# Two heads side by side in the array: neighbourhood units of a pair of heads and two-head score products in a hybrid encoder kernel

## The chip, the cores and the metric

The kernel runs on one core of a Trainium2 chip. The metric is device time in microseconds (us), the median of some runs; beside it there is one execution taken by the hardware profiler. Engines: PE is the tensor engine (its matmuls), DVE the vector engine, ACT the scalar engine, POOL and SP mainly issue transfers here. PSUM is the memory that PE writes; it has eight banks of 512 floats in each of 128 partitions.

## What is computed

Two layers over 512 tokens of width 1024 in float32. Each layer is a half-step SwiGLU feed-forward, a mixer with two kinds of heads, and a second feed-forward; a final norm follows.

```python
def hybrid_layer(x, ...):
    x = x + 0.5 * swiglu(rmsnorm(x, ffn1_norm), ffn1_wg, ffn1_wu, ffn1_wd)
    proj = rmsnorm(x, mix_norm) @ w_in          # all heads' q, k, v, gates
    na_o = rmsnorm(merge_heads(neighbourhood_attention(...)), na_gain)
    o_fwd = gla_chunked(qg, kg, vg, log_gf, True)
    o_bwd = flip(gla_chunked(flip(qg), flip(kg), flip(vg), flip(log_gb), False))
    gla_o = merge_heads(rmsnorm(o_fwd + o_bwd, gla_gain)) * silu(g_r)
    x = x + concatenate([na_o, gla_o]) @ w_out
    return x + 0.5 * swiglu(rmsnorm(x, ffn2_norm), ffn2_wg, ffn2_wu, ffn2_wd)
```

Neighbourhood attention has 8 heads of width 64: a query on the 8 x 64 grid of tokens sees a window of 8 x 16, with a learned bias per head, and a softmax over it. Gated linear attention (GLA) has 4 heads with keys of width 64 and values of width 128; the score of a query and a key is their product, damped by the gates between them, in both directions.

## The kernel before

Every activation lies with its features on the 128 partitions and the 512 tokens along the row. A projection is done as three products of rounded high and low parts (`mm3`, L165), with the weight quarters split by ACT and DVE shortly before (`split`, L144). These products, 0.23 us apart at 512 columns, are the bulk of the work.

The mixer (`mixer`, L530) emits four streams that `interleave` (L502) puts in one order, by what each step says it takes on PE and how long its successor must wait: `gla_all(0)` and `gla_all(1)` for the two pairs of GLA heads, `na_all` for the neighbourhood heads, and `fillers`, the projections of the next heads and then the first part of the output projection. LVL, SCL, NAP are such waiting times, in planned us. A scheduler in the framework then moves instructions of each engine once more within what dependencies allow, so that the order on an engine isn't quite that of the code.

Two heads share a tile of q and k: head 0 of the pair in partitions 0 to 63, head 1 in 64 to 127. A product for one head thus fills 64 of PE's 128 rows.

GLA (`gla_levels`, L596) builds its scores in levels. For the levels up to 64 tokens, `scores` (L625) takes for one head eight products of 64 x 64 (`blocks`, L619, L623), with odd blocks in the lower half of the output's partitions, and merges them into `atc` by a masked copy on DVE (L633), or by ACT for the first and the last level (L630, L688). Between levels four DVE products (L659, L660, L665, L666) scale keys and queries by the gates. The 128 level is four products of 128 columns a head (L697), the 256 level two halves of two products of 256 columns (L711); ACT copies them out (L700, L715).

A neighbourhood unit (`na_unit`, L828) is half of the query columns of one head: two score products of 256 columns (L846), bias and maximum on DVE (L851), exponentials on ACT (L855), the division (L860), four transposes (L864), ACT's copy out (L866), and four products with the values that write 64 partitions of the tile `po` (L874). Its bias comes by two POOL transfers a head (L834, L835). `na_all` (L890) keeps up to three units in flight.

PSUM is divided into pools: four banks "mm" for the projections, two banks "sc" for all scores, one "tp" for transposes and row sums, one "o" for `po`. A score step of one head takes one of the two "sc" banks and gives it back when its scores are read.

Every fp32 product is two records in the trace: a step of eight products shows as x16.

Of the kernel before, what the change touches and what calls it, by code (L numbers as in the profile page):

```python
# [9 lines left out]
F32 = mybir.dt.float32  # L10
# [15 lines left out]
SCL = 1.31  # L26
HEAD = 9
# [5 lines left out]
NAP = 5.46  # L33
# [27 lines left out]
def trunk_kernel(ctx, tc, xin, wgu, wdn, win, wcode, wgate, wout, vec, rpbt,  # L61
# [68 lines left out]
    # the tensor engine's clock comes up while the first data are on their way  # L130
# [106 lines left out]
    def rsqrt_row(ps, n, t, r, a, act=False):  # L237
        # 1/sqrt(mean + eps): exp(-ln/2) as a start, then one Newton step
# [116 lines left out]
    def ffn(l, which):  # L355
# [27 lines left out]
        def direct_pairs(hid):  # L383
            # the first weight tiles, while the row scales are on their way
# [93 lines left out]
    def last_row(pss, hs):  # L478
        # the last two chunks and the row scales of the final norm, for one half of the tokens
# [50 lines left out]
    def mixer(l):  # L530
# [3 lines left out]
        # gate codes: both parts of the weights side by side, summed by the gate product  # L534
# [11 lines left out]
        def codes():  # L546
            # both copies of the codes; then the first as high parts, the second as low parts
# [48 lines left out]
        def gla_levels(pr):  # L596
# [22 lines left out]
            def blocks(ps, op):  # L619
                # the eight blocks of 64 tokens, odd ones in the lower half of the rows  # L620
                for i in range(8):
                    o = (i % 2) * 64
                    PE.matmul(ps[o:o + 64, (i // 2) * 64:(i // 2 + 1) * 64], *op(i), start=True, stop=True)  # L623

            def scores(hh, kk, qf, li):  # L625
                ps = psum("sc")
                blocks(ps, lambda i: (kk[hh * 64:hh * 64 + 64, i * 64:(i + 1) * 64], qf(i)))
                dst = atc[:, hh * H2:(hh + 1) * H2]
                if li is None:
                    S.activation(dst, ps[:, :H2], AF.Copy)  # L630
                else:
                    m = lms[:, li, :].rearrange("p (a t) -> p a t", a=1).broadcast_to([P, 4, 64])
                    V.copy_predicated(dst.rearrange("p (b t) -> p b t", b=4), m,  # L633
                                      ps[:, :H2].rearrange("p (b t) -> p b t", b=4))

            for hh in range(2):
                scores(hh, ka, lambda i: qa[hh * 64:hh * 64 + 64, i * 64:(i + 1) * 64], None)
                yield 0.7, SCL
            for hh in range(2):
                scores(hh, ka, lambda i: qop(hh, i, 1), 0)  # L640
                yield 0.7, SCL
            for li, h in enumerate((1, 2, 4, 8, 16, 32, 64, 128)):
# [25 lines left out]
                if h2 <= 32:  # L668
                    for hh in range(2):
                        scores(hh, kc, lambda i: qop(hh, i, h2), li + 1)  # L670
                        yield 0.7, SCL
                elif h2 == 64:
                    for hh in range(2):
                        b = hh * 64
                        ps = psum("sc")

                        def halves(i):
                            kk, qq = (KF, QF) if i % 2 == 0 else (KB, QB)
                            return (kk[b:b + 64, i * 64:(i + 1) * 64],
                                    qq[b:b + 64, (i ^ 1) * 64:((i ^ 1) + 1) * 64])  # L680

                        blocks(ps, halves)
                        at.append(sl("at", F32, f"g{pr}"))
                        av = at[hh].rearrange("p (b two t) -> p two b t", b=4, two=2)
                        for o in range(2):
                            rows = slice(o * 64, o * 64 + 64)
                            for src, k in ((atc[rows, hh * H2:(hh + 1) * H2], o), (ps[rows, :H2], 1 - o)):
                                S.activation(av[rows, k], src.rearrange("p (b t) -> p b t", b=4), AF.Copy)  # L688
                        yield 0.7, SCL
                elif h2 == 128:  # L690
                    for hh in range(2):
                        b = hh * 64
                        ps = psum("sc")
                        for s in range(4):
                            t = s ^ 1
                            kk, qq = (KF, QF) if s < t else (KB, QB)
                            PE.matmul(ps[:, s * P:(s + 1) * P], kk[b:b + 64, s * P:(s + 1) * P],  # L697
                                      qq[b:b + 64, t * P:(t + 1) * P], start=True, stop=True)
                        g["m", hh] = sl("am", F32, f"g{pr}")
                        S.activation(g["m", hh], ps, AF.Copy)  # L700
                        yield 0.9, SCL
                else:
                    for hh in range(2):
                        b = hh * 64
                        for half in range(2):
                            ps = psum("sc")
                            kk, qq = (KF, QF) if half == 0 else (KB, QB)
                            o = 256 * (1 - half)
                            for j in range(2):
                                s = 2 * half + j  # L710
                                PE.matmul(ps[:, j * 256:(j + 1) * 256],  # L711
                                          kk[b:b + 64, s * P:(s + 1) * P], qq[b:b + 64, o:o + 256],
                                          start=True, stop=True)
                            g["f", hh, half] = sl("af", F32, f"g{pr}")
                            S.activation(g["f", hh, half], ps, AF.Copy)  # L715
                        yield 1.8, 0.5
# [65 lines left out]
        # neighbourhood attention  # L782
        def vmat_steps(pss, src, tags):
            # the values with the tokens as rows: the chunks' token blocks times two weight tiles
# [43 lines left out]
        def na_unit(hp, hh, jp, ctxd):  # L828
            hd = 2 * hp + hh
            b = hh * 64  # L830
            q, k = got["qk", hp]
            if jp == 0:
                nb0, nb1 = sl("nb", F32, "na"), sl("nb", F32, "na")
# [303 lines left out]
```

## Time and profile before

| | |
|---|---|
| median of three runs | 1989.24 us (1986.94 to 1990.84) |
| profiled execution, span | 1989.2 us |
| PE busy | 1969.5 us |
| DVE busy | 1423.7 us |
| ACT busy | 1025.6 us |
| TensorE clock granted, mean | 0.996 of full speed |

The profiled execution's span is that of all its instructions; the runs around it have the same time. A share of busy time is a mean over feed-forward and mixer stages. The mixer of layer 0 lies between some 362 and 658 us, that of layer 1 between 1342 and 1639.

### The profile page before, as it was taken

To read this page: it belongs to the slowest core of one execution; us is meant where nothing else is said; L and a number is where in the kernel's file an instruction comes from. 1 tells how busy PE (TensorE), PEld (TensorE's weight loads), DVE (VectorE), ACT (ScalarE), POOL (GpSimd) and SP (SyncE) were. 2 spreads that over 40 slices of the span, in tenths; PEclk is the share of its full clock that TensorE was granted. 3 is DMA by queue.
4 is the path that set the end of the run, shared out by engine and by line. 5 is a ranking of instruction groups with operands and counts; after the bars stand their busy time and mean duration, and the time that the engine had idled before them with its cause. 6 is when DMAs were issued, how large, how long until landed. Compare 5 with 4: busy or idle time off the path is not lost.

```text
span 1989.2 us, 32211 instructions
## 1 busy us (share of the span) xinstructions
PE 1969.5 (99%) x12490; PEld 1717.5 (86%) x12490; DVE 1423.7 (72%) x2745; ACT 1025.6 (52%) x1959; POOL 17.5 (1%) x36
## 2 busy tenths in 40 slices
PE   8999999999999999999999999999999999999997
PEld 7889999878778898999889898988777888999896
DVE  6958767666549985967787596775664689769585
ACT  5535535455555552644555364554554555536364
POOL 0000000000000000000000000000000000000000
PEclk9999999999999999999999999999999999999999
DMA  4332323222112332232223232223221133323322
GB/s 152 113 109 101 107 98 109 93 72 68 65 38 65 118 109 93 105 107 101 97 100 106 90 105 104 101 93 106 78 70 35 46 101 103 107 100 110 108 78 74
DMA packets 57737, 185.69 MB, mean 93 GB/s; under 512 B 6640, under 2 KB 13296, under 8 KB 45296
## 3 DMA queue, kind: packets, MB, share of 16 engines
q1 hardware_dynamic: 29904, 132.07, 19.4%
q10 hardware_dynamic: 25632, 45.27, 7.0%
q0 software_dynamic: 2048, 6.29, 1.0%
q8 instruction: 98, 1.61, 0.3%
q14 instruction: 55, 0.45, 0.1%
HBM read 181.51 MB, written 2.10 MB: 92 GB/s over the span
## 4 chain that ended last, share of the span: by engine, by line
PE 97%; DVE 1%; DMA 1%; ACT 0%; issue 0%; DVEq 0%; ACTq 0%
PE F_mm L166 14%; PE F_mm L168 14%; PE F_mm L167 14%; PE F_sc L166 9%; PE F_sc L167 9%; PE F_sc L168 9%; PE M_mm L166 6%; PE M_mm L168 6%; PE M_mm L167 6%; PE M_sc L623 2%; PE M_o L874 2%; PE M_sc L846 2%; PE M_tp L864 1%; PE M_sc L711 1%; PE M_mm L768 1%; DMA wraw<-in_wgu 0%
## 5 line engine op out<-in xcount | busy, mean ns | idle before, releaser
L146 ACT ACTIVATE F_wh<-F_wraw 128x512 fp32r<-128x512 f32 (+1 forms) x472 | 290.3, 618 | 453.7 <-PE F_sc L167 242.2
L166 PE MATMUL F_mm<-F_xc,F_wh 128*128 128x256 f32 x1792 | 500.7, 282 | 1.7 <-ACT F_wh L146 1.7
L167 PE MATMUL F_mm<-F_xc,F_wh 128*128 128x256 f32 x1792 | 501.5, 281 | 0.0
L168 PE MATMUL F_mm<-F_xc,F_wl 128*128 128x256 f32 x1792 | 495.0, 282 | 0.0
L147 DVE TENSOR_TENSOR F_wl<-F_wraw,F_wh 128x512 fp32r<-128x512 f32 (+1 forms) x472 | 313.3, 670 | 154.3 <-ACT F_wh L146 149.2
L166 PEld LDWEIGHTS F_mm<-F_xc,F_wh 128*128 128x128 f32 x1792 | 339.3, 190 | 4.3 <-ACT F_wh L146 2.5
L167 PEld LDWEIGHTS F_mm<-F_xc,F_wh 128*128 128x128 f32 x1792 | 340.3, 190 | 1.9
L168 PEld LDWEIGHTS F_mm<-F_xc,F_wl 128*128 128x128 f32 x1792 | 335.6, 190 | 0.0
L166 PE MATMUL F_sc<-F_hid,F_wh 128*128 128x512 f32 (+1 forms) x716 | 275.6, 387 | 1.3 <-DVE xt L452 1.3
L167 PE MATMUL F_sc<-F_hid,F_wh 128*128 128x512 f32 (+1 forms) x716 | 276.6, 386 | 0.0
L168 PE MATMUL F_sc<-F_hid,F_wl 128*128 128x512 f32 (+1 forms) x716 | 276.4, 386 | 0.0
L146 ACT ACTIVATE F_wh<-F_ws 128x512 fp32r<-128x512 f32 x256 | 162.3, 634 | 166.7 <-PE F_mm L167 106.9
L147 DVE TENSOR_TENSOR F_wl<-F_ws,F_wh 128x512 fp32r<-128x512 f32 x256 | 174.9, 688 | 41.8 <-ACT F_wh L146 38.6
L166 PEld LDWEIGHTS F_sc<-F_hid,F_wh 128*128 128x128 f32 x716 | 134.5, 188 | 28.9 <-DVE xt L452 3.0
L168 PEld LDWEIGHTS F_sc<-F_hid,F_wl 128*128 128x128 f32 x716 | 134.5, 188 | 26.5
L167 PEld LDWEIGHTS F_sc<-F_hid,F_wh 128*128 128x128 f32 x716 | 134.6, 188 | 25.7
L452 DVE SCALAR_TENSOR_TENSOR xt<-F_sc,xt 128x512 f32<-128x512 f32 x94 | 65.0, 692 | 97.0 <-PE F_sc L168 96.4
L166 PE MATMUL M_mm<-F_xd,M_wh 128*128 128x512 f32 x304 | 122.2, 403 | 0.0
L167 PE MATMUL M_mm<-F_xd,M_wh 128*128 128x512 f32 x304 | 120.6, 398 | 0.0
L168 PE MATMUL M_mm<-F_xd,M_wl 128*128 128x512 f32 x304 | 120.5, 397 | 0.0
L147 DVE TENSOR_TENSOR M_wl<-M_wraw,M_wh 128x512 fp32r<-128x512 f32 (+1 forms) x112 | 73.4, 668 | 36.3 <-ACT M_wh L146 23.1
L146 ACT ACTIVATE M_wh<-M_wraw 128x512 fp32r<-128x512 f32 (+1 forms) x112 | 67.7, 615 | 55.4 <-PE M_mm L167 37.6
(327 smaller groups left out, 3247.5 us busy)
## 6 DMA issues: line engine op xcount, KB each, us to landing
F_wraw<-in_wgu SPq DMA_DIRECT2D x64, 1024.0 KB, 4.8
F_wraw<-in_wdn SPq DMA_DIRECT2D x32, 1024.0 KB, 4.9
M_wraw<-in_win ACTq DMA_DIRECT2D x88, 256.0 KB, 3.6
F_wraw<-in_wgu ACTq DMA_DIRECT2D x80, 256.0 KB, 3.6
F_wraw<-in_wdn SPq DMA_DIRECT2D x16, 768.0 KB, 4.2
M_nb<-in_rpbt POOLq DMA_DIRECT2D x16, 256.0 KB, 3.0
M_wraw<-in_wout SPq DMA_DIRECT2D x16, 256.0 KB, 2.7
xt<-in_xin SPq DMA_DIRECT2D x8, 256.0 KB, 5.0
```

The lines of the kernel that those rows point to most:

```text
L146: S.activation(h, src, AF.Copy)
L147: V.tensor_tensor(l, src, h.bitcast(F32), op=ALU.subtract)
L166: PE.matmul(ps, wh, rh, start=first, stop=False, skip_group_check=more)
L167: PE.matmul(ps, wh, rl, start=False, stop=False, skip_group_check=more)
L168: PE.matmul(ps, wl, rh, start=False, stop=last, skip_group_check=more)
L452: V.scalar_tensor_tensor(xt[:, c, :], pss[j], 0.5, xt[:, c, :], ALU.mult, ALU.add)
L623: PE.matmul(ps[o:o + 64, (i // 2) * 64:(i // 2 + 1) * 64], *op(i), start=True, stop=True)
L711: PE.matmul(ps[:, j * 256:(j + 1) * 256], kk[b:b + 64, s * P:(s + 1) * P], qq[b:b + 64, o:o + 256], start=True, stop=True)
L768: PE.matmul(dst, vs(2 * half + j), fa[:, o:o + P], start=False, stop=(j == 1))
L846: PE.matmul(pss[:, jj * 256:(jj + 1) * 256], q[b:b + 64, j * P:(j + 1) * P], krhs, start=True, stop=True)
L864: PE.transpose(pt[:, i * P:(i + 1) * P], pp[:, i * P:(i + 1) * P], idn)
L874: PE.matmul(po[b:b + 64, j * P:(j + 1) * P], got["v", hp][VSEL[j][c]][:, hh * 64:(hh + 1) * 64], pT[:, (jj * 2 + c) * P:(jj * 2 + c + 1) * P],
```

## The change

All score steps, and the whole neighbourhood unit, are done for two heads at once. In `blocks` the two heads alternate product by product, each with its own "sc" bank; the masked copies follow for both. The 128 and 256 levels do the same. A neighbourhood unit is now half of the query columns of both heads of a pair (`na_unit(hp, jp, ...)`): four score products that alternate between the heads, then both softmaxes, two groups of transposes, and eight value products that alternate between the upper and the lower half of `po`. There are eight units a layer in place of sixteen. The bias of a unit is loaded one unit ahead by `na_load` into the very tile that DVE then writes the biased scores to; the copy of `po` into `nao` is gone, and the split and the squares read the bank. NAP, now for two heads, is 10.4 in place of 5.46; FAL, NAX and NAT are further planned waits.

```diff
-NAP = 5.46
+NAP = 10.4
+FAL = 1.4
+NAX = 0.0
+NAT = 0.3
...
-            def blocks(ps, op):
+            rows = slice(0, 64), slice(64, P)
+            def blocks(pss, op):
                 for i in range(8):
                     o = (i % 2) * 64
-                    PE.matmul(ps[o:o + 64, (i // 2) * 64:(i // 2 + 1) * 64], *op(i), start=True, stop=True)
-            def scores(hh, kk, qf, li):
-                ps = psum("sc")
...
+                    for hh in range(2):
+                        PE.matmul(pss[hh][o:o + 64, (i // 2) * 64:(i // 2 + 1) * 64], *op(hh, i),
+                                  start=True, stop=True)
+            def scores(kk, qf, li):
+                pss = psum("sc"), psum("sc")
+                blocks(pss, lambda hh, i: (kk[rows[hh], i * 64:(i + 1) * 64], qf(hh, i)))
+                for hh, ps in enumerate(pss):
+                    dst = atc[:, hh * H2:(hh + 1) * H2]
...
                 if h2 <= 32:
-                    for hh in range(2):
-                        scores(hh, kc, lambda i: qop(hh, i, h2), li + 1)
-                        yield 0.7, SCL
+                    scores(kc, lambda hh, i: qop(hh, i, h2), li + 1)
+                    yield 0.8, SCL
...
                 elif h2 == 128:
+                    pss = psum("sc"), psum("sc")
+                    for s in range(4):
+                        t = s ^ 1
+                        kk, qq = (KF, QF) if s < t else (KB, QB)
+                        for hh in range(2):
+                            PE.matmul(pss[hh][:, s * P:(s + 1) * P], kk[rows[hh], s * P:(s + 1) * P],
+                                      qq[rows[hh], t * P:(t + 1) * P], start=True, stop=True)
...
+                    for half in range(2):
+                        pss = psum("sc"), psum("sc")
...
+                            for hh in range(2):
+                                PE.matmul(pss[hh][:, j * 256:(j + 1) * 256],
+                                          kk[rows[hh], s * P:(s + 1) * P], qq[rows[hh], o:o + 256],
                                           start=True, stop=True)
...
+        def na_load(hp, jp):
+            pps = []
+            for hh in range(2):
+                pp = sl("pp", F32, "na")
+                nc.gpsimd.dma_start(pp, rpbt[l, 2 * hp + hh, :, jp * H2:jp * H2 + T])
+                pps.append(pp)
+            return pps
+        def na_unit(hp, jp, pps, ctxd):
             q, k = got["qk", hp]
+            sco = psum("sc"), psum("sc")
...
             for jj in range(2):
                 j = 2 * jp + jj
+                for hh in range(2):
...
+                    PE.matmul(sco[hh][:, jj * 256:(jj + 1) * 256], q[rows[hh], j * P:(j + 1) * P], krhs,
+                              start=True, stop=True)
+            for ps, pp in zip(sco, pps):
+                sm = small(4)
+                for jj, cs in enumerate(halves):
+                    V.tensor_tensor_reduce(pp[:, cs], ps[:, cs], pp[:, cs],
...
+                V.tensor_scalar(sm[:, 0:2], sm[:, 0:2], -1.0, None, ALU.mult)
+                for jj, cs in enumerate(halves):
+                    S.activation(pp[:, cs], pp[:, cs], AF.Exp, bias=sm[:, jj:jj + 1],
...
+            for pp in pps:
+                pt = psum("tp")
+                for i in range(4):
+                    PE.transpose(pt[:, i * P:(i + 1) * P], pp[:, i * P:(i + 1) * P], idn)
+                S.activation(pp, pt, AF.Copy)
+                yield 0.6, NAT
...
+                    v = got["v", hp][VSEL[j][c]]
+                    for hh in range(2):
+                        PE.matmul(po[rows[hh], j * P:(j + 1) * P], v[:, rows[hh]],
+                                  pps[hh][:, (jj * 2 + c) * P:(jj * 2 + c + 1) * P],
+                                  start=(c == 0), stop=(c == 1))
...
-                V.tensor_copy(nao := sl("nao", F32, "na"), po)
-                osplit(nao, hp, lvec(l, hp))
+                osplit(po, hp, lvec(l, hp))
```

What stands in a row on the engines, at the places that the prediction speaks of. A row is line, operation, output tile<-inputs, shape and repetition; tiles carry a running number, and line numbers are each program's own.

PE before, one GLA level of the second pair in layer 0: `M_sc` is a score bank, one for each head, `M_ga` and `M_kt` hold the scaled queries and keys, `M_mm` is a filler's bank.

```order
L864 MATMUL M_tp_4892<-con,M_pp_4781 128x128 x4
L623 MATMUL M_sc_4902<-M_ga_4649,M_kt_4772 64x64 x8
L623 MATMUL M_sc_4936<-M_ga_4649,M_kt_4772 64x64 x8
L167 MATMUL M_mm_4853<-M_wl_4837,F_xd_3611 128x256
L168 MATMUL M_mm_4853<-M_wh_4836,F_xd_3611 128x256
```

The same level after the change, on PE, as far as its fourth piece (the alternation goes on in ones up to eight blocks a head).

```order
L169 MATMUL M_mm_4776<-M_wh_4771,F_xd_3827 128x256
L170 MATMUL M_mm_4776<-M_wl_4772,F_xd_3827 128x256
L630 MATMUL M_sc_4868<-M_ga_4630,M_kt_4744 64x64 x2
L630 MATMUL M_sc_4869<-M_ga_4630,M_kt_4744 64x64 x2
L630 MATMUL M_sc_4868<-M_ga_4630,M_kt_4744 64x64
L630 MATMUL M_sc_4869<-M_ga_4630,M_kt_4744 64x64
```

The sixteen blocks of the two heads were eight and eight; now they alternate.

PE before, the last 64-token level of the second pair, layer 0: `M_tp` is the transpose bank; some 25 more rows of fillers follow before the 128 level (L697).

```order
L168 MATMUL M_mm_5747<-F_xd_3834,M_wl_5764 128x512
L623 MATMUL M_sc_5692<-M_ga_4649 64x64 x8
L728 MATMUL M_tp_5784<-con,M_vt_5725 128x128
L623 MATMUL M_sc_5728<-M_ga_4649 64x64 x8
L728 MATMUL M_tp_5784<-con,M_vt_5725 128x128 x3
L166 MATMUL M_mm_5748<-F_xd_3834,M_wh_5770 128x512
```

The same place after: L701 is the 128 level, L715 the 256 level, L876 transposes and L887 value products of the last neighbourhood unit.

```order
L171 MATMUL M_mm_5801<-F_xd_3834,M_wl_5824 128x512
L630 MATMUL M_sc_5700<-M_ga_4630 64x64 x8
L630 MATMUL M_sc_5701<-M_ga_4630 64x64 x8
L876 MATMUL M_tp_5734<-con,M_pp_5501 128x128 x4
L701 MATMUL M_sc_5865<-M_ga_4630 128x128 x4
L701 MATMUL M_sc_5866<-M_ga_4630 128x128 x4
L876 MATMUL M_tp_5750<-con,M_pp_5503 128x128 x4
L887 MATMUL M_o_5762<-M_pp_5501,M_vm_4993 64x128
L715 MATMUL M_sc_6005<-M_ga_4630 128x256 x2
L715 MATMUL M_sc_6006<-M_ga_4630 128x256 x2
```

The last filler stands ahead of the three levels, which now follow each other with a group of transposes or a single product between them.

ACT at that place after the change: L693 fills the tiles `M_at` from the score banks and from `M_atc`, L705 and L720 copy the 128 and 256 levels out, L877 the transposes.

```order
L693 ACTIVATE M_at_5718<-M_sc_5700 64x4x64 x2
L693 ACTIVATE M_at_5723<-M_atc_4633 64x4x64 x2
L693 ACTIVATE M_at_5723<-M_sc_5701 64x4x64 x2
L877 ACTIVATE M_pp_5501<-M_tp_5734 128x512
L705 ACTIVATE M_am_5875<-M_sc_5865 128x512
L705 ACTIVATE M_am_5877<-M_sc_5866 128x512
L877 ACTIVATE M_pp_5503<-M_tp_5750 128x512
L720 ACTIVATE M_af_6011<-M_sc_6005 128x512
L720 ACTIVATE M_af_6013<-M_sc_6006 128x512
```

The second head's bank is read after six of the copies; before, the copies from `M_atc` stood earlier in ACT's order and only four stood here.

## Rows read from the trace of the kernel before

**Rows 1.** The page: busy time by engine (share, instructions); the chain by engine

```profile
PE 1969.5 (99%) x12490; PEld 1717.5 (86%) x12490; DVE 1423.7 (72%) x2745; ACT 1025.6 (52%) x1959; POOL 17.5 (1%) x36
...
PE 97%; DVE 1%; DMA 1%; ACT 0%; issue 0%; DVEq 0%; ACTq 0%
```

**Rows 2.** Stretches: us; busy of PE, PEld, DVE, ACT, POOL; clock; DMA share; GB/s

```profile
400.00:500.00 100.00, 100.00 (x824) 79.74 (x823) 63.66 (x201) 55.16 (x129) 4.29 (x8) 1.00 0.22 69
500.00:590.00 90.00, 90.00 (x607) 68.14 (x606) 44.40 (x123) 45.20 (x92) 2.15 (x4) 1.00 0.17 57
590.00:658.00 68.00, 67.91 (x339) 56.87 (x338) 56.12 (x93) 37.02 (x65) 0.00 (x0) 1.00 0.24 78
```

**Rows 3.** Chain of work, layer 0: start us, us until the next piece, what

```profile
408.19 0.81 PE M_sc L623 x16
...
415.93 1.06 PE M_sc L846 x4
...
434.51 1.02 PE M_o L874 x8
...
453.92 0.91 PE M_sc L623 x30
...
539.81 1.08 PE M_sc L697 x8
...
565.92 0.61 PE M_sc L623 x16
...
570.67 0.23 PE M_mm L167
...
572.97 1.64 PE M_sc L697 x16
...
581.43 1.92 PE M_sc L711 x8
```

**Rows 4.** Timeline of PE around a score group: start us, us, instruction

```profile
415.53 0.28 PE L167 MATMUL M_mm<-M_wl,F_xd 128*128 128x256 f32 x1
415.65 0.28 PE L168 MATMUL M_mm<-M_wh,F_xd 128*128 128x256 f32 x1
415.86 1.13 PE L846 MATMUL M_sc<-M_k,M_q 64*128 64x256 f32 x4
416.91 0.50 PE L166 MATMUL M_mm<-F_xd,M_wh 128*128 128x512 f32 x1
417.25 0.40 PE L167 MATMUL M_mm<-F_xd,M_wh 128*128 128x512 f32 x1
```

**Rows 5.** Timeline of PE where two heads' score steps meet

```profile
454.30 0.22 PE L623 MATMUL M_sc<-M_ga,M_kt 64*64 64x64 f32 x1
454.31 0.22 PE L623 MATMUL M_sc<-M_gq,M_gk 64*64 64x64 f32 x1
```

**Rows 6.** Timeline of PE where a 128 level meets a neighbourhood group

```profile
534.93 0.82 PE L697 MATMUL M_sc<-M_ga 64*128 64x128 f32 x5
535.49 0.48 PE L846 MATMUL M_sc<-M_k,M_q 64*128 64x256 f32 x1
535.59 0.38 PE L697 MATMUL M_sc<-M_ga 64*128 64x128 f32 x2
```

**Rows 7.** The page's DMA issues: the bias, count, KB each, us to landing

```profile
M_nb<-in_rpbt POOLq DMA_DIRECT2D x16, 256.0 KB, 3.0
```

**Rows 8.** Timeline of DVE: two passes over a head's neighbourhood scores

```profile
469.35 0.42 DVE L851 CUSTOM_DVE_ANT_0 M_pp<-M_sc,M_nb 128x256 f32<-128x256 f32 x1
...
469.70 0.42 DVE L851 CUSTOM_DVE_ANT_0 M_pp<-M_sc,M_nb 128x256 f32<-128x256 f32 x1
```

**Rows 9.** Timeline of DVE: first and last of a level's four products

```profile
566.57 0.43 DVE L659 TENSOR_TENSOR M_ga<-M_ga,M_pk 128x256 f32<-128x256 f32 x1
...
567.58 0.42 DVE L666 TENSOR_TENSOR M_ga<-M_ga,M_pk 128x256 f32<-128x256 f32 x1
```

**Rows 10.** Timeline of ACT: four copies of a 64-token step

```profile
565.71 1.67 ACT L688 ACTIVATE M_at<-M_sc 64x256 f32<-64x256 f32 x4
```

More of the change, by code (lines that the diff above doesn't have):

```diff
@@ L642, in gla_levels @@
+            scores(ka, lambda hh, i: qa[rows[hh], i * 64:(i + 1) * 64], None)
+            yield 0.8, SCL
+            scores(ka, lambda hh, i: qop(hh, i, 1), 0)
+            yield 0.8, SCL
             for li, h in enumerate((1, 2, 4, 8, 16, 32, 64, 128)):
@@ L668, in gla_levels, with halves @@
                 if h2 <= 32:
-                    for hh in range(2):
-                        scores(hh, kc, lambda i: qop(hh, i, h2), li + 1)
-                        yield 0.7, SCL
+                    scores(kc, lambda hh, i: qop(hh, i, h2), li + 1)
+                    yield 0.8, SCL
                 elif h2 == 64:
[L673 to L682, printed above, removed]
+                    pss = psum("sc"), psum("sc")
+                    def halves(hh, i):
+                        kk, qq = (KF, QF) if i % 2 == 0 else (KB, QB)
+                        return (kk[rows[hh], i * 64:(i + 1) * 64],
+                                qq[rows[hh], (i ^ 1) * 64:((i ^ 1) + 1) * 64])
+                    blocks(pss, halves)
+                    for hh, ps in enumerate(pss):
                         at.append(sl("at", F32, f"g{pr}"))
@@ L690, in gla_levels @@
+                    yield 0.8, SCL
                 elif h2 == 128:
-                    for hh in range(2):
[L692 to L698, printed above, removed]
+                    pss = psum("sc"), psum("sc")
@@ L701, in gla_levels @@
-                        yield 0.9, SCL
-                else:
[L703 to L712, printed above, removed]
+                        S.activation(g["m", hh], pss[hh], AF.Copy)
@@ new lines, in gla_levels @@
+                    yield 1.0, SCL
+                else:
+                    for half in range(2):
+                        pss = psum("sc"), psum("sc")
+                        kk, qq = (KF, QF) if half == 0 else (KB, QB)
+                        o = 256 * (1 - half)
+                        for j in range(2):
+                            s = 2 * half + j
+                            for hh in range(2):
+                                PE.matmul(pss[hh][:, j * 256:(j + 1) * 256],
+                                          kk[rows[hh], s * P:(s + 1) * P], qq[rows[hh], o:o + 256],
@@ new lines, in na_unit @@
+            for sm, pp in zip(sms, pps):
+                V.reciprocal(sm[:, 2:4], sm[:, 2:4])
+                for jj, cs in enumerate(halves):
+                    V.tensor_scalar(pp[:, cs], pp[:, cs], sm[:, 2 + jj:3 + jj], None, ALU.mult)
+            yield 1.0, NAX
+            for pp in pps:
[4 more added lines that the diff above has]
+                yield 0.6, NAT
@@ L869, in na_unit @@
+            if jp == 0:
                 ctxd["po"] = psum("o")
@@ L884, in na_unit @@
                 else:
-                    sq = sl("sq", F32, "na")
+                    sq = sl("sq", F32, "ws")
                     S.activation(sq, po, AF.Square)
                     V.tensor_tensor(st["nacc"], st["nacc"], sq, op=ALU.add)
-            yield 0.9, 0.0
+            yield 1.1, 0.0
         def na_all():
             ctxd = {}
-            act = []
-            for u in range(16 + DEEP):
-                if u < 16:
-                    hp = u // 4
-                    yield ("qk", hp)
-                    yield ("v", hp)
-                    act.append(na_unit(hp, (u // 2) % 2, u % 2, ctxd))
-                left = NAP
-                for gq in act[::-1]:
-                    y = next(gq, None)
-                    if y is not None:
-                        left -= sum(y)
-                        yield y
-                act = act[-DEEP:]
+            units = []
+            pps = na_load(0, 0)
+            for u in range(8 + DEEP):
+                if u < 8:
+                    yield ("qk", u // 2)
+                    yield ("v", u // 2)
+                    units.append(na_unit(u // 2, u % 2, pps, ctxd))
+                left = NAP if u < 8 else 3.0
+                for age, n in enumerate((1, 2, 1)):
+                    if 0 <= u - age < 8:
+                        for _ in range(n):
+                            y = next(units[u - age])
+                            left -= sum(y)
+                            yield y
+                if u < 7:
+                    pps = na_load((u + 1) // 2, (u + 1) % 2)
                 yield 0.0, max(left, 0.0)
```

85 lines of the change are left out of this document (23 added, 62 removed).

## The prediction

> **What bounds the kernel now.** I read the page first: TensorE (PE) is busy for 99% of the span and the chain of work that ended last runs on PE for 97% of it [rows 1]. Then the table of stretches, because only the mixer is touched: between 400 and 658 us (layer 0, whose mixer starts at some 362 us; layer 1 is the same 980 us later) PE is busy for all but 0.1 us, while DVE is at 49 to 83% and ACT at 50 to 55% [rows 2]. So in the stage that changes the time is the sum of PE's start-to-start steps, and whatever shortens these shortens the run until another engine comes late. The chain gives that sum directly: a piece of the chain is the time from the first start of a group to the first start of what follows [rows 3].
>
> Two things are to be seen in these pieces. First, a small group pays for changing the shape of the array. In [rows 4] products with 256 columns start every 0.12 us, but 0.21 us pass before the first product of 64 rows; after it the first full one holds PE for 0.34 us, where such products otherwise take 0.23 [rows 3]. That is about 0.09 + 0.11 us on the neighbours of each small group, beside a late first step and a late last step that its own piece contains. Second, products in different parts of the array run together already. A step of one head (16 records of 64x64) takes 0.61 us; two heads that happen to stand back to back take 0.91 and not twice 0.61 [rows 3], and where the first head's last blocks meet the second head's first, records of both start within 0.01 us [rows 5]. The same holds for row halves with 128 columns: a neighbourhood product starts at 535.49 while the level products of the other half go on every 0.11 us, and two heads of L697 take 1.64 instead of twice 1.08 [rows 3, 6]. Two products of the same half don't: L711 x8 takes 1.92 against 1.06 for the four records of the same shape in L846 [rows 3].
>
> **The change, part by part (both layers).** In the reordered program the two heads alternate product by product in nearly all steps, so I take a two-head step at the price of the one-head step.
>
> GLA steps of 64x64. Before: 64 one-head steps, 8 of them with the strided operand of the first level at 0.81, the others 32 alone at 0.61 and 24 in 12 adjacent pairs at 0.91: 6.5 + 19.5 + 10.9 = 36.9 us. After: 32 steps; 26 at 0.62, 4 strided at 0.82, and 2 (the last level of the second pair, where the order has eight blocks of one head and then eight of the other) at 0.91: 16.1 + 3.3 + 1.8 = 21.2. Saved 15.7.
>
> Neighbourhood scores. 32 groups at 1.06 become 16 of the same length: saved 17.0.
>
> Values (L874). 32 groups at 1.02 = 32.6. After, the two heads fill the two column halves, so 16 groups of eight products need 1.02 each where they stand whole; the order cuts ten of them into 1 + 7 and two into 3 + 5, and a cut costs about 0.36: 16 x 1.02 + 12 x 0.36 = 20.6. Saved 12.0. The trace before has no two 128x64 products of different column halves next to each other. The bounds are 0, if they run one after another (then 11 us of the 12 stay), and the full 12; I take the full value, since the blocks of L623 also go to alternating column halves of one bank and start in pairs.
>
> Levels 128 and 256. L697: eight one-head groups, four alone at 1.08 and two adjacent pairs at 1.64, 7.6 us; after, two at 1.64 (four products of one head, then four of the other) and two better mixed at about 1.35: 6.0. L711: 16 half-level groups, 16.5 us with their adjacent ones (eight at 1.06, two runs of 1.92, the rest 4.2); after, the order leaves eight groups of one head alone, with fillers between the heads, at 1.06, and pairs four: 12.7. Saved 1.6 + 3.8.
>
> Neighbours. The number of changes between the full array and a small shape falls from 124 to 86 by the order: 38 x 0.19 = 7 us.
>
> Sum: 15.7 + 17.0 + 12.0 + 1.6 + 3.8 + 7 = 57 us less for PE.
>
> Off PE: the eight copies of the finished head pair out of its bank go (0.69 us of DVE each), and the bias is loaded into the tile that becomes the probabilities. That makes 32 loads of 256 KB in place of 16 of that size and 16 of half; they land in 3.0 us [rows 7] and are issued a unit, some 16 us of PE work, ahead. I cost both at nothing; what hides the loads is that distance, and without it each unit would pay up to 3 us.
>
> **What comes late next.** PE takes its instructions in order, so a product that waits holds all fillers behind it. Every two-head step now needs both score banks, so both heads of the step before must have been read. In the middle of the mixer the order leaves 3.2 to 5 us of PE work between such steps. Reading two neighbourhood heads takes four DVE passes that start 0.34 us apart [rows 8], about 1.9 us with the hand-overs; that fits unless DVE is behind. I put 1 us per layer on it, bounds 0 and 5.
>
> The end of the second pair's levels is different. Before, some six us of fillers lie between the 64-token step and the 128 step (565.92 and 572.97), and between that and the 256 step (581.43) [rows 3]. In the new order the fillers are used up by then, and 0.7 us of PE work separates the first two and 0.7 us the next. But each level first needs four DVE products on the result of the one before, 1.4 us from first start to last end [rows 9], and the 128 step needs both banks, for which ACT has six copies of 0.4 us in its queue [rows 10]: 2.4 us. So PE waits about 2 us at the first place and 1 at the second. ACT is then behind by the copies of all these steps: two table loads and two SiLU passes stand in its queue before the first square of the gated output, whose row sums PE wants 3 us after it made the products; I put 2 us there and 1 on the row scales of the neighbourhood part. With the middle: 7 us a layer, 14 in all, bounds 4 and 28.
>
> **Sum.** The profiled execution took 1989.2 us, and the median of the runs is 1989.24, so no correction is needed: 1989 - 57 + 14 = 1946.
>
> **Rivals.**
> (1) The waits are shorter than I think: fillers slide under them and only some 3 us come back. 1935. For: PE stood still nowhere in the mixer before [rows 2]. Against: at the end of the levels nothing is left to slide.
> (2) The sharing of the array is incomplete. A one-head step starts a record every 38 ns (0.61 / 16), a two-head step of 0.62 would start one every 19, and the trace shows two heads sharing the array over some 0.2 us only [rows 5]. If a step costs the 0.91 of two adjacent heads, 26 x 0.29 = 8 us come back; if the values don't pair, 11. 1954 to 1965.
> By the Trainium skill (TensorE: Matmul & The Clock Gate, on the gap of 56 ns) starts never come closer than about 25 ns; the trace differs, with starts under 10 ns apart [rows 5]. By that rule a 32-record step would take about 0.9 us and the sum would be the 1954 of this rival.
> (3) Slower, by one mechanism: the bank hand-over in the score pool. There are 60 two-head steps, and with both banks in every step nothing can be scored while either head is still being read. If DVE is on average so late that each step waits 1.2 us, 60 x 1.2 = 72 us come back and the run takes 1932 + 72 = 2004; it decides from 0.95 us a step. For: DVE already works at 64% in this stretch and its work is pressed into about 15% less time [rows 2]. Against: the distances in the order are twice the reading time, and the next stretch ran at 83% without holding PE up.
> The Trainium skill has that rule too (TensorEngine Tiling (Array Packing), PSUM Bottleneck): tiling speeds the array but not the reading of PSUM, which may become the bound. The trace bears it out only so far as the reading time above goes.
> (4) No change: the pace is set by the chain of a neighbourhood unit (scores, exponentials, transposes, values), planned at 10.4 us for two heads against 2 x 5.46 before. Its eight units would still allow some 8 us less, 1981, or with waits 1989. Against: before, PE and not this chain was full.
>
> **How the numbers follow.** Forecast (waits of 4 to 28 us) 0.58; rival 1 0.12; rival 2 0.16; rival 3 0.07; rival 4 0.07, half of it within 0.2%. Changes of 0.2%, 4 us, are about what can be told from none. Faster 0.89, same 0.04, slower 0.07. The range must leave out the slow ends of rivals 2 to 4: 1930 to 1966.
>
> **What would show it.** The mixer's stretch of 296 us should shrink by about 21 us a layer; groups of L853 should stay near 1.06 for eight records, L630 steps near 0.62 for 32, L887 near 1.02 for 16. Waits of PE should stand at the 128 and 256 steps of the second pair and before the first row sum of the gated output. It is wrong if L887 takes 1.9 (no pairing), if L630 takes 0.9, or if PE waits for DVE at the scores in the middle of the mixer.

## The result, and the profile after

The changed kernel takes 1956.83 us (1953.4 to 1957.71), before it 1989.39: a ratio of 0.9835, 95% interval 0.9822 to 0.9849. It is 32.6 us faster. The forecast was 1946, 43 us faster, in a range of 1930 to 1966; so the time lies in the range, and 11 us of the forecast gain are missing.

The page of the changed kernel, as [rows 1] of before: busy time by engine, and the chain of work that ended last by engine.

```profile
PE 1924.7 (98%) x12490; PEld 1687.4 (86%) x12490; DVE 1416.9 (72%) x2705; ACT 1020.1 (52%) x1959; POOL 17.4 (1%) x36
...
PE 97%; DVE 1%; DMA 1%; ACT 1%; issue 0%; DVEq 0%; ACTq 0%
```

PE's busy time fell by 44.8 us, but the span only by 33.7 (1989.2 to 1955.5): PE now stands still for some 11 us more. Where it does is read from the table of stretches (as [rows 2]: busy us and instructions of PE, PEld, DVE, ACT, POOL, then granted clock, DMA share, GB/s). The transposes that follow layer 0's mixer now start 15 us earlier (643.64, before 658.91), and layer 1's mixer is 20 us shorter; some 21 a layer had been forecast. The last two rows are of layer 1.

```profile
400.00:500.00 100.00, 100.00 (x968) 81.42 (x967) 70.95 (x207) 61.82 (x143) 4.28 (x8) 1.00 0.28 91
...
545.00:556.00 11.00, 8.94 (x74) 6.38 (x73) 6.62 (x15) 7.19 (x15) 0.00 (x0) 0.92 0.29 97
556.00:563.00 7.00, 7.00 (x42) 5.00 (x43) 1.06 (x2) 3.91 (x7) 0.00 (x0) 0.64 0.00 0
...
580.00:590.00 10.00, 7.39 (x49) 6.34 (x48) 8.83 (x15) 7.18 (x14) 0.00 (x0) 1.00 0.05 15
590.00:600.00 10.00, 9.59 (x35) 7.77 (x36) 9.16 (x17) 1.71 (x4) 0.00 (x0) 0.83 0.04 13
600.00:629.00 29.00, 26.50 (x110) 21.22 (x109) 25.69 (x44) 14.65 (x27) 0.00 (x0) 0.95 0.28 91
...
1515.00:1520.00 5.00, 3.58 (x54) 2.95 (x53) 2.63 (x6) 4.89 (x12) 0.00 (x0) 1.00 0.27 87
1520.00:1525.00 5.00, 5.00 (x25) 3.30 (x25) 1.43 (x4) 2.17 (x5) 0.00 (x0) 0.51 0.16 52
```

In the middle of the mixer PE is as full as before, with DVE at 71% where it had 64%. At the end two things are new: PE is idle, and in the stretches with or behind the idle places the granted clock is below full, as low as 0.51, which is the lower of its two levels, 1.2 of 2.4 GHz. Before, the clock was full in both mixers: [rows 2] for layer 0, and for layer 1 also behind the one wait of PE there, which is in the output projection (a wait and a stretch of the kernel before):

```profile
PE OP_mm L166 <- ACT OP_wh L146: 1.6, 1, 1.6
...
1600.00:1700.00 100.00, 98.40 (x453) 81.66 (x452) 84.98 (x148) 53.26 (x94) 0.00 (x0) 1.00 0.33 110
```

The steps themselves are as forecast. Chain of work of the changed kernel, as [rows 3] (start us, us until the next piece, what): two-head steps, the strided first level, and neighbourhood scores and values.

```profile
400.60 0.62 PE M_sc L630 x32
...
404.39 0.82 PE M_sc L630 x32
...
413.92 1.06 PE M_sc L853 x8
...
461.76 1.02 PE M_o L887 x16
...
487.24 1.02 PE M_o L887 x14
```

A balance over both mixers with their output projections, worked out from the matmul records: each step is the time from one record's start to the next, with idle times over 0.25 us counted apart. What the lower clock cost is the length of a stretch times what its granted clock lacks to 1: in layer 0 from the rows above 11 x 0.08 + 7 x 0.36 + 10 x 0.17 + 29 x 0.05 = 6.6 us, in layer 1 in the same way 5.2 us. PE is idle for only 0.1 us of the time at half clock, so this is a loss of the steps.

| us, both layers | before | changed | forecast of the difference |
|---|---|---|---|
| GLA steps of 64x64 | 37.8 | 21.9 | -15.7 |
| neighbourhood scores | 33.0 | 17.0 | -17.0 |
| values | 33.7 | 22.9 | -12.0 |
| 128 and 256 levels | 23.9 | 22.1 | -5.4 |
| everything else on PE | 443.3 | 443.8 | -7 |
| of these steps, lost to the lower clock | 0 | 11.8 | none |
| PE idle | 1.6 | 12.9 | +14 |
| sum | 573.3 | 540.6 | -43 |

At full clock the steps would be 527.7 - 11.8 = 515.9, which is 55.8 us less than before against 57 forecast. The idle time grew by 11.3, against 14. What is missing is the clock: 55.8 - 11.3 - 11.8 = 32.7, and the measured gain is 32.6.

Where PE waits (waits of PE in the changed kernel: waiter, releaser, us in total, times, the longest):

```profile
PE M_mm L169 <- ACT M_on L777: 6.0, 2, 3.0
...
PE M_sc L701 <- ACT M_at L693: 3.5, 3, 1.6
PE OP_mm L171 <- DVE OP_wl L150: 2.6, 2, 2.3
```

The second of these is the 128 step of the second pair. The chain of work there, layer 0:

```profile
546.39 3.98 DMA M_wraw<-in_wout
...
550.47 0.63 ACT M_wh L149
551.10 0.27 ACT M_at L693
...
553.04 0.39 ACT M_at L693
...
553.47 1.47 PE M_sc L701 x8
...
556.60 2.02 PE M_sc L715 x8
558.62 1.90 PE M_o L887 x14
...
561.34 1.07 PE M_sc L715 x8
```

The copies that the 128 step waits for are the ones forecast, some 2.4 us of them (three of the five pieces are left out). But they begin 1.4 us after the 64 step has ended (549.67 in the timeline): ahead of them on ACT stands the split of an output weight (L149), which starts when its transfer has ended. So only some 0.6 of the 2.1 us that PE waits here would be left without that split, an estimate from the two idle times there and this delay (1.56 + 0.50 - 1.43). The first L715 row behind the wait takes 2.02 and the L887 row 1.90, where the same groups took 1.07 at 561.34 and 1.02 at 487.24: half clock. Layer 0 is at half clock for 6.8 us here, which costs 3.4 us, more than the wait of 2.1.

The first of the three waits is at the gated output; the chain there:

```profile
587.43 0.69 ACT M_r L242
...
588.15 0.63 ACT M_r L243
588.78 0.61 ACT M_oh L152
589.39 0.48 ACT M_sq L776
589.87 0.50 ACT M_on L777
...
590.41 0.50 PE M_mm L169
```

PE waits for a bank of the fillers, in which a GLA head's output stands until ACT has squared and copied it (L776, L777); these two stand behind the row scales and the split of the head before. The table loads and SiLU passes of the prediction ran some 20 us earlier (timeline of ACT):

```profile
564.65 1.28 ACT L744 ACT_TABLE_LOAD   x1
565.94 1.15 ACT L744 ACTIVATE M_gr<-M_gr 128x512 f32<-128x512 f32 x2
...
568.41 0.60 ACT L776 ACTIVATE M_sq<-M_mm 128x512 f32<-128x512 f32 x1
```

PE doesn't wait for the square that follows them: it has no idle time over 0.25 us between 563 and 587.4 us.

### The profile page after: what moved, and what is told of

It is laid out like the page before. It is cut to its first block, busy times and chain, and to the rows that moved or that the text cites. A ratio compares the mean times of both kernels' runs of the same rounds, so it can differ in the third digit from the quotient of the medians.

```text
span 1955.5 us, 32220 instructions
## 1 busy us (share of the span) xinstructions
PE 1924.7 (98%) x12490; PEld 1687.4 (86%) x12490; DVE 1416.9 (72%) x2705; ACT 1020.1 (52%) x1959; POOL 17.4 (1%) x36
## 4 chain that ended last, share of the span: by engine, by line
PE 97%; DVE 1%; DMA 1%; ACT 1%; issue 0%; DVEq 0%; ACTq 0%
PE F_mm L169 14%; PE F_mm L171 14%; PE F_mm L170 14%; PE F_sc L169 9%; PE F_sc L170 9%; PE F_sc L171 9%; PE M_mm L169 6%; PE M_mm L170 6%; PE M_mm L171 6%; PE M_o L887 1%; PE M_sc L630 1%; PE M_tp L876 1%; PE M_sc L853 1%; PE M_mm L773 1%; PE M_sc L715 1%; DMA wraw<-in_wgu 0%
## 5 line engine op out<-in xcount | busy, mean ns | idle before, releaser
L149 ACT ACTIVATE F_wh<-F_wraw 128x512 fp32r<-128x512 f32 (+1 forms) x472 | 289.5, 617 | 439.9 <-PE F_sc L170 238.8
L169 PE MATMUL F_mm<-F_xc,F_wh 128*128 128x256 f32 x1792 | 500.5, 282 | 1.3 <-ACT F_wh L149 1.3
L169 PEld LDWEIGHTS F_mm<-F_xc,F_wh 128*128 128x128 f32 x1792 | 339.3, 190 | 3.7 <-ACT F_wh L149 1.9
L169 PE MATMUL F_sc<-F_hid,F_wh 128*128 128x512 f32 (+1 forms) x716 | 275.6, 387 | 1.3 <-DVE xt L455 1.3
L149 ACT ACTIVATE F_wh<-F_ws 128x512 fp32r<-128x512 f32 x256 | 161.8, 632 | 170.0 <-PE F_mm L170 109.8
L169 PEld LDWEIGHTS F_sc<-F_hid,F_wh 128*128 128x128 f32 x716 | 134.6, 188 | 29.0 <-DVE xt L455 3.0
L169 PE MATMUL M_mm<-F_xd,M_wh 128*128 128x512 f32 x304 | 122.1, 403 | 0.0
L149 ACT ACTIVATE M_wh<-M_wraw 128x512 fp32r<-128x512 f32 (+1 forms) x112 | 67.6, 614 | 46.8 <-PE M_mm L170 37.9
```

The source lines that it names most:

```text
L149: S.activation(h, src, AF.Copy)
L169: PE.matmul(ps, wh, rh, start=first, stop=False, skip_group_check=more)
```

## The experiments

**e1_gla: the GLA half alone.** `gla_levels` as changed, everything for the neighbourhood part as before.

> Only the GLA half of the change: two-head levels, neighbourhood units of one head as before. Theory A (the change saves the 57 us of PE steps that were forecast, and the rest was lost at the end of the mixer, because there the two halves together use up all fillers): this half alone keeps fillers in its order between the last levels of the second pair, so it has no wait of PE over 0.5 us in the mixers and no stretch below full clock there; gain 15.7 + 1.6 + 3.8 + some 3 for the neighbours = 24 us, 1965 (1960 to 1970). Rival B (a fixed share of what is saved on PE comes back everywhere, since ACT and DVE do not get faster): 33/57 of 24 us, 1975.

Measured: 1983.45 us, 0.9967 of before (0.9956 to 0.9979). Neither figure. PE's steps, with what they lose to the lower clock taken out, are 21 us shorter than before, near the 24 of A, but PE is idle for 10.9 us, and that was to be none. The clock is at its lower level for 17 us of the mixers, 4.3 of them idle, so the steps lose some 6.4. Waits of PE, and the stretches where it waits:

```profile
PE M_tp L731 <- DVE M_ms L245: 3.0, 2, 1.5
...
PE M_tp L234 <- ACT M_sqh L147: 2.4, 2, 1.2
```

```profile
570.00:575.00 5.00, 3.27 (x16) 1.78 (x14) 3.35 (x7) 4.72 (x9) 0.00 (x0) 0.97 0.33 107
575.00:580.00 5.00, 2.79 (x7) 1.45 (x8) 3.32 (x5) 1.91 (x3) 0.00 (x0) 0.50 0.00 0
```

The row sums of the neighbourhood part and the transposes of GLA's last values share the one transpose bank here, at a place where nothing else is left for PE. So the loss at the end of the mixer doesn't need both halves.

**e2_na: the neighbourhood half alone.** `gla_levels` as before, everything else as changed.

> Only the neighbourhood half of the change: units of two heads, GLA levels of one head as before. Theory A: fillers still lie between the last levels, no wait and no fall of the clock; gain 17.0 + 12.0 + some 4 for the neighbours = 33 us, 1956 (1951 to 1962), as fast alone as both halves together, and the gains of the two halves sum to some 57, not to 33. Rival B: 33/57 of it, 1970.

Measured: 1978.81 us, 0.9948 (0.9933 to 0.9963); again neither. PE is idle for 2.8 us only and the clock stays up, so A is right on the waits. But the scores take 31.8 us where the whole change has 17.0; the values take 22.0, as there. The timeline around one unit shows why (start us, us, engine, instruction):

```profile
426.32 1.13 PE L851 MATMUL M_sc<-M_k,M_q 64*128 64x256 f32 x4
...
431.64 1.13 PE L851 MATMUL M_sc<-M_k,M_q 64*128 64x256 f32 x4
```

The four records of one head stand at 426.32, those of the other 5.3 us later: the scheduler has torn the unit's heads apart. 28 of the score groups have four records, 2 have eight; in the whole change all 16 have eight. The code alternates the heads in both. The gains of the halves, 6.8 and 11.4 us, sum to 18 and not to 33: the change is worth more than its parts.

**e10_pairbank: why the heads come apart.** The half of e2_na, with the two score banks handed out as one tile.

```diff
-            sco = psum("sc"), psum("sc")
+            both = scpair()
+            sco = both[:, 0, :], both[:, 1, :]
...
-                ps = psum("sc")
+                ps = scpair()[:, 0, :]
```

> The neighbourhood half alone, with the two score banks given out as one tile of two banks: a GLA step of one head, and every other user, takes both and gives both back. Theory C (in the neighbourhood half alone the two heads' score products were torn apart because one-head GLA steps take and return one bank at a time): all 16 score groups now stand whole at 1.06 us, 17 us of PE steps where the half alone had 31.8; values and GLA steps as there. PE will wait more, since no two one-head steps can overlap and the feed-forward shares these banks, so the mixers' PE steps decide and not the time: 1965 to 2000. Rival D (they are torn apart for another reason, late data of one head for instance): the score groups keep some 30 us.

Measured: all 16 score groups stand whole, as C has it. Chain of work, one of them:

```profile
431.40 1.06 PE M_sc L856 x8
```

Their steps sum to 19.7 us with a part at lower clock. So the banks that come free one at a time were the cause in the half. In the whole change every two-head step asks for both, and its groups stand whole; but they are still two separate banks, and with other orders the heads come apart there too (e3_serial, e9 below). The time, 2070.55 us (1.0412, 1.0394 to 1.0429), is worse than I allowed for: one-head steps with one pair of banks can't overlap, PE is idle for 33 us in the mixers, and the lower clock costs the steps some 28 more (32 of it by the table's reckoning, but PE is idle for 8.6 us of that time).

**e3_serial: without the alternation.** The whole change, with the loop over the heads outside in all five places, here the values:

```diff
-            for jj in range(2):
-                j = 2 * jp + jj
-                for c in range(2):
-                    v = got["v", hp][VSEL[j][c]]
-                    for hh in range(2):
+            for hh in range(2):
+                for jj in range(2):
+                    j = 2 * jp + jj
+                    for c in range(2):
+                        v = got["v", hp][VSEL[j][c]]
```

> The whole change, but in each two-head step the products of the first head come first and then those of the second (eight and eight, four and four, two and two), in place of one and one. If sharing the array needs the alternation: L630 steps near the 0.91 of two adjacent heads, score groups of the neighbourhood near 1.4 to 1.6 in place of 1.06, values near 1.6 to 1.9 in place of 1.02, together 20 to 30 us more of PE steps. If it is enough that both heads stand next to each other in the queue: the same 0.62, 1.06 and 1.02. The order at the end of the mixer also changes, so the prices decide and not the time alone: 1965 to 1985 by the first, 1945 to 1957 by the second.

Measured: 1981.08 us, 0.9957 (0.9942 to 0.9972), as by the first. Chain of work:

```profile
443.76 0.91 PE M_sc L630 x30
...
464.39 1.06 PE M_sc L853 x4
...
513.91 1.51 PE M_o L887 x16
```

A GLA step takes 0.91 and not 0.62, values that stand whole 1.51 and not 1.02. The score groups I had at 1.4 to 1.6; 24 of 28 stand alone with four records at 1.06, so in this order the heads are apart again, though every step asks for both banks. The other four stand whole and take 1.07 with starts in pairs 13 ns apart: for them the loop order made no difference (the trace doesn't name the heads, so it doesn't say whether the scheduler put them in ones). What is shown is that the blocks of 64x64 and the values need the alternation. With both effects, PE's steps at full clock are some 37 us longer than with it (552.7 against 515.9).

**e7_warm: the wait filled with nothing.** The whole change, with nine useless products before the first real one into a bank that waits for its data:

```diff
             po = psum(tag)
+            if hd == 0:
+                for _ in range(9):
+                    PE.matmul(po, onr, XD[0][0], start=True, stop=True)
```

> The whole change, plus nine full-array products of 512 columns in each layer that compute nothing (their bank is overwritten), which the order places in front of the 128 step of the second pair, where PE waited 2.1 us (layer 0) and 1.4 us (layer 1). They take 9 x 0.23 = 2.1 us, all the wait or a little more. Theory A1 (the fall of the granted clock after the wait is a cost of its own, 3.4 us in each layer): with PE kept busy the clock stays at 1.0 through the 128 and 256 steps, and the run is 4 to 7 us faster although it does more work: 1950 to 1953. Rival A2 (the levels are held up by ACT's copies and DVE's products whatever PE does, so that the slow stretch would only turn into waits): 1956 to 1959.

Measured: 1953.13 us, 0.9817 (0.9803 to 0.9832), against 0.9835 for the whole change: 3.7 us faster with 4.1 us more work on PE (18 products of 0.23). By the time alone this is just outside A1, nearer to it than to A2, and the intervals of the two ratios overlap; what decides is the clock. The same stretches as above and two pieces of the chain (the values' line is L890 here):

```profile
545.00:556.00 11.00, 10.65 (x84) 7.71 (x82) 6.42 (x15) 7.61 (x16) 0.00 (x0) 1.00 0.30 97
556.00:563.00 7.00, 7.00 (x63) 5.71 (x62) 3.16 (x7) 5.74 (x12) 0.00 (x0) 1.00 0.01 2
```

```profile
556.49 1.07 PE M_sc L715 x8
557.56 1.02 PE M_o L890 x14
```

The clock stays at 1.00 (0.92 and 0.64 without these products), and the 256 step takes 1.07, not 2.02. At the gated output PE still waits, 2.4 us in each layer, and the clock still falls; layer 1's output projection now waits 2.3 us, with a fall of its own. In all the steps still lose 6.6 us to the lower clock. The products fill the wait with full-array work, so this run doesn't tell the idle time from the small products around it; at the gated output only full-array products stand around the wait, and the clock falls there too.

**e5_swap and e8_before_swap: another projection first.**

```diff
-         ('gv2', 'gv3'),
          ('gv0', 'gv1'),
+         ('gv2', 'gv3'),
```

> The whole change, with one pair of projections moved: the values of the first two GLA heads (gv0, gv1) are projected before those of the last two. The outputs of the first GLA pair and their row sums can then stand between the last levels of the second pair, with some 40 fillers behind the 128 step. Theory A: the waits of 2.1 and 1.4 us at the 128 step and the half-clock stretches after them go (some 10 us over both layers), and most of the 3.0 us waits at the gated output with theirs: 1935 to 1946. Rival B or one where DVE and ACT limit the end of the mixer anyway: the waits move elsewhere, 1950 to 1960.

> The kernel before the change, with gv0/gv1 projected before gv2/gv3, the move that gained 10 us on the changed kernel. By theory A it gains only where PE waits, and before the change PE waits nowhere in the mixer: 1987 to 1993. If the move has a value of its own (shorter products, less switching), it gains some us here too: 1980 to 1986.

Measured: on the changed kernel 1946.77 us, 0.9782 (0.9766 to 0.9798), 10 us better; on the kernel before 1992.75, 1.0019 (1.0009 to 1.0028), 3 us worse. So the move has no value of its own. On the changed kernel it puts output products of the first pair between the last levels, and the waits at the 128 step and at L169 are gone; new ones of 1.1 and 1.5 us come at the row sums and transposes behind them, and the steps lose 6.1 us to the lower clock in place of 11.8. The idle time is hardly less, 10.7 us in place of 12.9, so the clock is the larger part of the 10 us. The time on the changed kernel is just above A's range and below B's.

**e6_gvfirst, e9_gvfirst104 and e11_nap85: more cover at the end.** e6 projects both pairs of GLA values before the output gates, lets the planner emit GLA's output products without waiting for the gates, and sets NAP to 8.5; e9 is e6 with NAP as in the change; e11 is the change with NAP alone altered:

```diff
-NAP = 10.4
+NAP = 8.5
```

> The whole change, with the order of the last projections changed (both pairs of GLA values first, then the output gates), the output products of GLA no longer waiting in the planner for the gates, and NAP 8.5 in place of 10.4, so that the neighbourhood part ends earlier. In the order fillers, or output products of GLA, now stand in front of each of the last levels, and the row sum of the neighbourhood scales is followed by 30 output products. Theory A: all of what is lost at the end of the mixer (11 us of added waits and 12 us of half clock in the changed kernel) can go: no wait of PE over 1 us in the mixer, 1930 to 1940. Rival B (ACT and DVE set the end of the mixer): 1944 or more, no better than the swap alone.

> As the run before, but with NAP left at 10.4: tells the order of the projections from the planned time of the units. By theory A the late row sums of the neighbourhood part come behind the last levels again, with waits of 1 to 3 us there: 1936 to 1946. By rival B as the run before.

> The whole change with one constant altered, NAP 8.5 in place of 10.4. Theory A: nine fillers then stand between the last 64 step and the 128 step, and the last values before them, so the wait at the 128 step and its half-clock stretch shrink or go, while those at the gated output remain: 1946 to 1953. Rival B (ACT and DVE set the end of the mixer): 1955 to 1958.

Measured: e6 1935.96 us, 0.9731 (0.9715 to 0.9747), as A has it; e9 1956.26, 0.9835 (0.9821 to 0.9850), B's time, and no better than the change; e11 1933.37, 0.9716 (0.9701 to 0.9730), better than A's range. So the order of the projections, with the gates' place in the planner, brought nothing by itself in e9, where four pairs of waits remain and 4 of 16 score groups are torn apart again (21.2 us); NAP brought it all. B falls with e11: ACT and DVE do the same work there. Its stretches, and its longest waits of PE inside the mixer:

```profile
545.00:556.00 11.00, 9.24 (x93) 6.68 (x93) 8.94 (x18) 10.54 (x23) 0.00 (x0) 1.00 0.19 64
556.00:563.00 7.00, 7.00 (x58) 6.47 (x57) 3.18 (x6) 6.63 (x11) 0.00 (x0) 1.00 0.15 54
563.00:580.00 17.00, 17.00 (x120) 15.62 (x119) 12.54 (x20) 8.89 (x16) 0.00 (x0) 1.00 0.03 9
```

```profile
PE M_tp L733 <- DVE M_ms L247: 1.3, 2, 0.6
PE M_tp L236 <- ACT M_sqh L149: 1.1, 2, 0.5
```

No wait there is longer than 0.7 us, the clock stays at 1.00, and PE's steps come to 512.0 us, 59.7 less than before. This one constant is worth 23 us on top of the change: the version that beats both kernels. A smaller NAP was not tried on the kernel before; PE waited only 1.6 us in both mixers there.

## Why the prediction was right, point by point

**What bounds the kernel.** Right: PE's start-to-start steps set the time, and the middle of the mixer shows no wait of PE in either kernel. The bias loads, costed at nothing, hold nothing up on PE: they land in 3.1 us, and no wait of PE is for their tiles.

**The terms on PE.** Right, and in size: 15.9 saved for 15.7 on the GLA steps, 16.0 for 17.0 on the scores, 10.8 for 12.0 on the values (12.8 in e11, where no value product runs at lower clock). The two heads share the array fully: L887 x16 at 1.02 is the step for which the trace before had no row. The 128 and 256 levels saved 1.8 in place of 5.4, in the main because part of the second pair's run at half clock; in e11 they save 9.9, as all eight half-levels stand there with both heads together, where the change has four so and eight groups of one head. The neighbours' 7 us is not seen by itself: the rest of PE's work is 0.5 longer in the changed kernel, with most of the lower clock in it, and 5.6 shorter in e11.

**Rival 2** is out: 32 records in 0.62 us start every 19 ns. The rule of the Trainium skill (TensorE: Matmul & The Clock Gate, "Wait — 56ns, not 53.3ns?"), no start closer than about 25 ns, would have made it 0.8 by an estimate from that figure (the prediction has 0.9); the trace differs. The page gives it for products back to back, whatever their size; for products in different parts of the array it did not hold here. **Rival 3** is out as well: no score step in the middle waits, though DVE went from 64 to 71%. **Rival 1**, short waits, was right on the middle of the mixer only, which waits nothing for the 1 us per layer that I put there; **rival 4**, no change, is out with the verdict.

**What comes late next** is the step that failed, by its size and in part by its places. Of its five places one is as described: the 128 step waits 2.1 us in layer 0 and 1.4 in layer 1 (forecast 2), for ACT's copies. Even there the size is partly luck, since in layer 0 the copies start 1.4 us late behind the split of an output weight, which the forecast didn't have. The wait at the gated output is 3.0 (forecast 2), but not before its first row sum and not behind the table loads and SiLU passes: it comes some 20 us after these, at a bank that ACT has yet to empty. The middle of the mixer, the 256 step and the row scales of the neighbourhood part wait nothing for the 1 us that I put at each; the 256 step waits nothing in e7_warm either, at full clock. In their place the output projection waits for its weights' split (2.3 and 1.1 us; before, 1.6 in layer 1). That the sum, 11.3 us more than before, is near the 14 is therefore luck in part.

The larger fault is that each wait was priced as its own length alone. The granted clock falls after it, and that costs as much again, 11.8 us. No row of the mixers before showed it, since PE waited only once there, 1.6 us, and the clock stayed at 1.00; e7_warm shows it, because there the clock stays up with the same copies ahead. With the clock the term is 23 us, inside its bounds of 4 to 28.

**The cause behind it**, fillers that run out before the last levels, was named in the prediction and is borne out by e11_nap85: with the neighbourhood units planned closer, nine fillers stand between the last 64 step and the 128 step (548.25 to 550.50 us), the row sums of the neighbourhood part come at 552 and not at 571, and from 576 us on the output projection's products stand around the last row sums of the gated output.

What stays open: why the planned 10.4 us of a unit came out as some 18 on PE (units at 413.92, 425.65, 447.41 us and so on) was not tried apart from NAP itself, and why the scores are torn apart in part in e9 is not known. The clock's fall was taken away by e7, e6 and e11, but what besides the wait decides on it is open, as the last section shows.

## What to carry to other kernels

When PE is full, a change that shortens PE's work also takes away the work that hides the other engines; look in the new order for the places where nothing is left to stand between two dependent steps, and price the waits there at between once and twice their length, since the clock may fall behind them: in the changed kernel 12.9 us of idle time went with 11.8 us lost to the clock, in e3_serial 8.8 with 4.8, in e11, where no wait is over 0.8, 5.6 with nothing. A planner's constants belong to the change: a time that was right for the longer work cost 23 us here. For the small blocks and the values, sharing the array fully needs both heads' products next to each other in the order, one and one. Whether they stay there depends on who else takes their banks: one-head users tear them apart, and while the two are separate banks the scheduler may still do so.

## What the runs showed of the hardware

The same wait can leave the clock alone or not. In e3_serial PE waits 3.05 us at 599 us and 3.07 at 1574.5, behind the same work. Stretches behind the first and the second:

```profile
600.00:605.00 5.00, 2.51 (x11) 2.09 (x12) 4.96 (x9) 2.28 (x5) 0.00 (x0) 1.00 0.00 0
605.00:610.00 5.00, 5.00 (x24) 4.12 (x23) 5.00 (x10) 1.41 (x3) 0.00 (x0) 1.00 0.08 25
...
1575.00:1580.00 5.00, 2.44 (x6) 1.96 (x7) 4.97 (x9) 2.34 (x5) 0.00 (x0) 0.69 0.01 3
1580.00:1585.00 5.00, 5.00 (x16) 3.92 (x15) 4.22 (x8) 0.42 (x1) 0.00 (x0) 0.63 0.00 0
```

In layer 0 the granted clock stays at 1.00, in layer 1 it falls. In the changed kernel a wait of 1.42 us in layer 1 was enough, while 1.6 us in the kernel before and 1.67 in e2_na left the clock at 1.00. So the loss behind a single wait is not to be had to the microsecond from the wait's length.
